# MLP down product: the running sums of seven chunks move from SBUF and VectorE to DRAM and accumulating DMAs

## The chip, the cores and the metric

The kernel runs on one core of a Trainium2 chip. The metric is the device time of one execution in microseconds (us); lower is better. Before the change the median of three runs was 2839.44 us (2832.86 to 2839.78).

Engines: PE is TensorE (matmuls, results in PSUM), DVE is VectorE, ACT is ScalarE, POOL is GpSimd, SP is SyncE, which here only issues DMAs. Every engine works through its own instructions in a fixed order; an instruction that waits holds back all behind it on that engine. A DMA is issued by an engine and lands later, while the engine goes on.

## The reference

Two layers, each a token mixer (mLSTM in layer 0, gated DeltaNet in layer 1), a cross-attention and an MLP, each wrapped as x + RMSNorm(f(RMSNorm(x))). There are 256 tokens of width 2048. The change lies in the MLP:

```python
D_MODEL = 2048; SEQ = 256; DEPTH = 2; D_FF = 4 * D_MODEL

def sq_relu_mlp(h, w_up, w_down):
    u = jax.nn.relu(h @ w_up)
    return (u * u) @ w_down

    # in reference(), for each layer i
        h = rms_norm(x, g[4])
        x = x + rms_norm(sq_relu_mlp(h, w_up[i], w_down[i]), g[5])
```

## The kernel before

**Numbers.** Products are made in float32r; weights and activations are split in two parts, hi and lo, and a product is hi x hi + hi x lo + lo x hi. For each piece of weights SP loads it to a raw tile, ACT casts it to `hi` (L154, L93, L94, L86) and DVE subtracts to get `lo` (L155, L82). These pieces are taken in a planned order (`Weights.plan`); each is called a unit here. Three units are kept: a unit's `hi` buffer is free when PE has ended the unit three before it. A unit of the down product is 4 x 128 rows by 512 columns of `w_down`: 12 matmuls for each of the two blocks of 128 tokens, 24 in all.

**The MLP** (`mlp`, L1132) cuts the 8192 features of the middle layer in NQ = 8 chunks. The up product of chunk 0 comes first (L1137). Then a loop over c = 1 to 7, called passes 1 to 7, does two things at once: the up product of chunk c (L1147 to L1153, eight feature blocks f) and the down product of chunk c - 1. The last chunk's down product stands behind the loop (`out_proj` in layer 0, `prod_tok` with `last` in layer 1).

The down product of a pass has two parts. For the first 1024 output columns it is a seven-product scheme for 2 x 2 blocks: seven products, `m0` to `m6`, each 128 x 512 in a PSUM bank of its own (five banks of tag "acc", two of tag "ps"), built up by L1164 to L1166 between the feature blocks. At f = 6 the first three are complete, at f = 7 the other four. For the other 1024 columns, `prod_tok("down", ..., 2, ...)` (L1178) makes an ordinary product: 2 column blocks x 2 token blocks, four banks, 4 units.

So each pass yields eleven 128 x 512 results, which are summed over the seven passes: in pass 1 ACT copies them to SBUF (L1170 for the seven, `Post.add` L616 for the four), in passes 2 to 7 DVE adds them from PSUM to SBUF (L1172, L616). The sums live in `y` (four tiles of two blocks, the eight blocks of the MLP's output) and in three tiles of tag "pair", which has three buffers. In pass 7 seven more additions on DVE (L1177) turn the seven sums into four output blocks. Behind the loop the last chunk's product is added to the same `y` blocks (L616), which are squared on ACT (L308), scaled and added to x.

The order on each engine is made by a scheduler from the order of the program and the dependencies.

Of the kernel before, what the change touches and what calls it, by code (L numbers as in the profile page):

```python
# [7 lines left out]
F32 = mybir.dt.float32  # L8
F32R = mybir.dt.float32r
AF = mybir.ActivationFunctionType  # L10
ALU = mybir.AluOpType
# [3 lines left out]
P = 128  # L15
# [165 lines left out]
def trunk(ctx: ExitStack, tc, x, mem, norm_g, mem_norm_g, w_mem_kv, w_xq, w_xo, w_up, w_down,  # L181
          mlstm_w_in, mlstm_b_gates, mlstm_head_g, mlstm_w_out, gdn_w_in, gdn_conv_w, gdn_a_log,
          gdn_dt_bias, gdn_norm_g, gdn_w_out, out):
    nc = tc.nc
    V, S, G, PE = nc.vector, nc.scalar, nc.gpsimd, nc.tensor
# [4 lines left out]
    tmp = ctx.enter_context(tc.tile_pool(name="tmp", bufs=2))  # L190
# [81 lines left out]
    def psum(name):  # L272
        return ps.tile([P, 512], F32, tag="ps", bufs=3, name=name)

    def acc(name):
        return ps.tile([P, 512], F32, tag="acc", bufs=5, name=name)
# [491 lines left out]
    first = []  # L768
# [239 lines left out]
    def out_proj(key, y, post, free, plus=False, more=None):  # L1008
        post.more = more
        prod_tok(key, y, 4, lambda ch, t, a: post.take(ch, t, a, plus), post=post, free=free)  # L1010
        return post.advance()
# [67 lines left out]
    def mlp_bias(rms):  # L1079

        s2 = small.tile([P, 2], F32, tag="s2", name="s2")
        V.tensor_scalar(s2, rms.sums(), 1.0 / D, EPS, ALU.mult, ALU.add)
        V.scalar_tensor_tensor(s2, s2, EPS, s2, ALU.mult, ALU.mult)
        return s2
# [47 lines left out]
    def mlp(l, lead):  # L1132
        mp_stack = ExitStack()
        mp = ws.tsum = mp_stack.enter_context(tc.tile_pool(name="mp", bufs=1))
        h = lead.h
        cur = Half(mp, 0, True)
        prod_feat("up", h, FK, cur.evac, lead=lead)  # L1137
        post = Post(l, 5, (1, 0) if l == 0 else None)
        y = post.y
        m = [tmp.tile([P, 512], F32, tag="pair", bufs=3, name=f"m{i}") for i in range(3)]  # L1140
        m1, m6, m7 = m
        c11, c21, c12, m5 = (y[ch][:, t, :] for ch in range(2) for t in range(2))
        kept = [m1, c11, c12, m5, m6, m7, c21]
        for c in range(1, NQ):
            nxt = Half(mp, c % 2, c < NQ - 1)
            banks = [acc(f"m{i}") for i in range(5)] + [psum(f"m{i}") for i in range(5, 7)]
            for f in range(FK):  # L1147
                hi, lo, nk, _ = ws.take("up")
                a = psum("up")
                for k in range(nk):  # L1150
                    PE.matmul(a, hi[k], h[k][:, :], start=(k == 0), stop=False, skip_group_check=True)  # L1151
                    PE.matmul(a[:, T:], lo[k], h[k][:, 0:T], start=False, stop=(k == nk - 1), skip_group_check=True)  # L1152
                nxt.evac(f, Bank(a, True))  # L1153
                j, part = f // 2, f % 2
                hi, lo, nf, _ = ws.take("down2")
                if part == 0:
                    lhs = [cur.block(2 * j, 0), cur.block(2 * j + 1, 0), cur.form(3, j)]
                    to = (0, 1, 2)
                else:
                    lhs = [cur.form(0, j), cur.form(1, j), cur.form(2, j), cur.block(2 * j + 1, 1)]  # L1160
                    to = (3, 4, 5, 6)
                for i in range(nf):
                    (sh, sl), a = lhs[i], banks[to[i]]
                    PE.matmul(a, sh, hi[i], start=(j == 0), stop=False)  # L1164
                    PE.matmul(a, sh, lo[i], start=False, stop=False)  # L1165
                    PE.matmul(a, sl, hi[i], start=False, stop=(j == FK // 2 - 1))  # L1166
                if j == FK // 2 - 1:
                    for i in to:
                        if c == 1:
                            S.copy(kept[i], banks[i])  # L1170
                        else:
                            V.tensor_tensor(kept[i], banks[i], kept[i], ALU.add)  # L1172
            if c == NQ - 1:
                for d, a, b, op in ((c11, c11, m1, ALU.add), (m6, m6, m1, ALU.add), (m7, m7, m6, ALU.add),
                                    (c21, m7, c21, ALU.subtract), (c12, c12, m6, ALU.add), (c12, c12, m5, ALU.add),
                                    (m5, m5, m7, ALU.add)):
                    V.tensor_tensor(d, a, b, op)  # L1177
            prod_tok("down", cur.u, 2, lambda ch, t, a: post.add(ch + 2, t, a, c == 1))  # L1178
            cur = nxt
        mp_stack.close()  # L1180
        u = cur.u
        post.bias = mlp_bias(lead.x_rms)
        if l == 0:
            return out_proj("down", u, post, (("h", 8), ("u", 0)), True)

        def last(ch, t, a):
            post.take(ch, t, a, True)
            if ch == 3:
                for i in range(4):
                    post.residual(i, t)  # L1190
                    (nc.sync if i % 2 else nc.scalar).dma_start(out[0, t * P : (t + 1) * P, i * 512 : (i + 1) * 512],
                                                                xk[i][:, t, :])

        prod_tok("down", u, 4, last, split=True)
# [446 lines left out]
    for l in range(2):  # L1641
        if l == 0:
            with tc.tile_pool(name="ml", bufs=2) as sc:
                y, post = mlstm(sc, h0, xrms, x_rest)
        else:
            ws.first = 400
            with tc.tile_pool(name="g0", bufs=1) as g0:
                y, post = gdn(g0, lead)
            ws.first = 0
        with tc.tile_pool(name="wx", bufs=1) as wx:  # L1650
            key, free = (("g_out", (("u", 8), ("u", 0))), ("m_out", (("h", 8), ("u", 0))))[l == 0]
            lead = out_proj(key, y, post, free, l == 1, wx)
            with tc.tile_pool(name="xa", bufs=2) as sc:
                lead = cross(sc, l, lead)
        lead = mlp(l, lead)
# [24 lines left out]
```

## Time and profile before

| What | Value |
|---|---|
| median of three runs | 2839.44 us (2832.86 to 2839.78) |
| the profiled execution | 2837.68 us, span 2835.9 us |
| granted PE clock | 0.997 |
| passes of layer 0 | 613 to 1161 us; a pass takes some 86 us |
| passes of layer 1 | end at 2784 us |
| HBM | 534.4 MB read, 25.2 MB written |

How to read it: the span goes from the first to the last instruction of the profiled execution; its own time holds some 2 us more. The page's share of an engine is an average over the run, so the stage that matters is looked at in windows. A row of a timeline has the start (us), the duration (us), the engine, the line, the operation and what it writes and reads; in brackets stands how long the engine was idle before and what ended that.

The weights use the DMA engines throughout the MLP:

```profile
q1 hardware_dynamic: 520000, 505.02, 58.8%
```

### The profile page before, as it was taken

What the parts mean: (1) busy time and instruction counts of PE and PEld (TensorE: products, weight loads), DVE (VectorE), ACT (ScalarE), POOL (GpSimd) and SP (SyncE); (2) the same over time, 40 slices, a digit from 0 to 9 for tenths busy, and PEclk for the clock granted to TensorE, in tenths of its full rate; (3) what the DMA queues carried; (4) which work ended last, traced back from release to release, by engine and by line L of the source; (5) the groups of instructions that cost most, each with busy time, mean ns of one, the idle gap of its engine ahead of it and who ended that gap; (6) DMA issues with size and microseconds to landing.
All of it is one profiled execution on the core that took longest, in us unless ns stands there. A gap on an engine that the chain in (4) does not pass through costs nothing.

```text
span 2835.9 us, 41595 instructions
## 1 busy us (share of the span) xinstructions
PE 2815.1 (99%) x15696; PEld 2396.1 (84%) x15696; DVE 2101.0 (74%) x3177; ACT 1672.4 (59%) x2603; POOL 170.4 (6%) x365
## 2 busy tenths in 40 slices
PE   9999999999999999999999999999999999999998
PEld 8888888888888888888888998888888888888887
DVE  6555657888888887787887895556578788888876
ACT  7444546776655566565765554544477666655663
POOL 0000000000000000002211114230000000000000
PEclk9999999999999999999999999999999999999999
DMA  8545565566666666757877778665654666666665
GB/s 281 181 147 176 193 200 165 169 194 195 198 196 195 199 189 195 227 155 232 244 220 222 213 209 276 200 202 194 204 178 151 211 184 202 193 193 193 195 194 168
DMA packets 537561, 562.34 MB, mean 198 GB/s; under 512 B 24672, under 2 KB 388016, under 8 KB 536080
## 3 DMA queue, kind: packets, MB, share of 16 engines
q1 hardware_dynamic: 520000, 505.02, 58.8%
q0 software_dynamic: 16464, 53.58, 5.8%
q8 instruction: 123, 2.02, 0.3%
q10 hardware_dynamic: 896, 1.09, 0.1%
q14 instruction: 78, 0.64, 0.1%
HBM read 534.38 MB, written 25.23 MB: 197 GB/s over the span
## 4 chain that ended last, share of the span: by engine, by line
PE 40%; DVE 6%; ACT 3%; DMA 2%; issue 2%; POOL 0%; DVEq 0%; ACTq 0%; POOLq 0%
PE up L1151 7%; PE up L1152 4%; DVE lo L155 2%; PE down L496 2%; PE down L497 2%; PE down L498 2%; PE g_out L497 2%; PE g_out L496 2%; PE g_out L498 2%; PE m L1165 2%; PE m L1164 2%; PE m L1166 2%; PE gz L496 1%; PE gz L498 1%; PE gz L497 1%
## 5 line engine op out<-in xcount | busy, mean ns | idle before, releaser
L155 DVE TENSOR_TENSOR lo<-raw,hi 128x1024 fp32r<-128x1024 f32 x812 | 966.3, 1220 | 327.7 <-ACT hi L154 324.9
L154 ACT CAST hi<-raw 128x1024 fp32r<-128x1024 f32 x812 | 827.1, 1047 | 479.6 <-PE down L498 96.7
L1151 PE MATMUL up<-h,hi 128*128 128x512 f32 x1792 | 636.9, 398 | 0.0
L1152 PE MATMUL up<-h,lo 128*128 128x256 f32 x1792 | 503.4, 281 | 0.4 <-DVE lo L155 0.4
L1151 PEld LDWEIGHTS up<-h,hi 128*128 128x128 f32 x1792 | 336.9, 188 | 82.4
L1152 PEld LDWEIGHTS up<-h,lo 128*128 128x128 f32 x1792 | 338.5, 189 | 5.3 <-DVE lo L155 0.8
L496 PE MATMUL down<-hi,u 128*128 128x512 f32 x576 | 224.2, 389 | 0.0
L497 PE MATMUL down<-lo,u 128*128 128x512 f32 x576 | 224.1, 389 | 0.0
L498 PE MATMUL down<-hi,u 128*128 128x512 f32 x576 | 224.1, 389 | 0.0
L82 DVE TENSOR_TENSOR lo<-tsum,hi 128x1024 fp32r<-128x1024 f32 x112 | 136.8, 1221 | 82.6 <-ACT hi L86 82.5
L86 ACT CAST hi<-tsum 128x1024 fp32r<-128x1024 f32 x112 | 117.6, 1050 | 131.9 <-PE up L1151 96.6
L496 PEld LDWEIGHTS down<-hi,u 128*128 128x128 f32 x576 | 108.1, 188 | 22.5
L498 PEld LDWEIGHTS down<-hi,u 128*128 128x128 f32 x576 | 108.1, 188 | 22.5
L497 PEld LDWEIGHTS down<-lo,u 128*128 128x128 f32 x576 | 108.1, 188 | 22.3
L93 ACT CAST hi<-raw 128x512 fp32r<-128x512 f32 x56 | 34.9, 623 | 121.6 <-PE up L1151 92.2
L1240 DVE SCALAR_TENSOR_TENSOR cv<-pad,cols,cv 128x256 f32<-128x256 f32 x192 | 92.5, 483 | 16.3 <-ACT cv L1238 12.4
L82 DVE TENSOR_TENSOR lo<-raw,hi 128x512 fp32r<-128x512 f32 x112 | 103.6, 955 | 0.0
L496 PE MATMUL gz<-hi,h 128*128 128x512 f32 x256 | 103.1, 403 | 0.0
L498 PE MATMUL gz<-hi,h 128*128 128x512 f32 x256 | 102.4, 400 | 0.0
L497 PE MATMUL gz<-lo,h 128*128 128x512 f32 x256 | 102.4, 400 | 0.0
L445 PE MATMUL gk<-h,hi 128*128 128x512 f32 x256 | 89.8, 395 | 0.0
L445 PE MATMUL gv<-h,hi 128*128 128x512 f32 x256 | 89.5, 394 | 0.0
(511 smaller groups left out, 6174.8 us busy)
## 6 DMA issues: line engine op xcount, KB each, us to landing
raw<-in_w_up SPq DMA_DIRECT2D x256, 512.0 KB, 4.7
raw<-in_w_down SPq DMA_DIRECT2D x256, 512.0 KB, 5.1
raw<-in_gdn_w_in SPq DMA_DIRECT2D x192, 512.0 KB, 4.9
raw<-in_mlstm_w_in SPq DMA_DIRECT2D x96, 512.0 KB, 4.0
raw<-in_gdn_w_out SPq DMA_DIRECT2D x64, 512.0 KB, 4.7
raw<-in_mlstm_w_out SPq DMA_DIRECT2D x32, 512.0 KB, 4.6
at_d<-at POOLq DMA_DIRECT2D x8, 1536.0 KB, 7.7
ab<-at_d POOLq DMA_DIRECT2D x16, 768.0 KB, 5.1
```

The source lines that it names most:

```text
L82: sub = lambda d, a, b: nc.vector.tensor_tensor(d, a, b, ALU.subtract)
L86: nc.scalar.copy(ht[:, j : j + 2, :], t[:, j : j + 2, :])
L154: a = nc.scalar.copy(h_, raw[:, :, :n])
L155: return a, nc.vector.tensor_tensor(l_, raw[:, :, :n], h_, ALU.subtract)
L445: PE.matmul(a, hi[k], srcs[k][:, :], start=(k == 0), stop=False, skip_group_check=True)
L496: PE.matmul(a, sh, hi[j], start=(kk == 0), stop=False)
L497: PE.matmul(a, sh, lo[j], start=False, stop=False)
L498: end[0] = PE.matmul(a, sl, hi[j], start=False, stop=(kk == nk - 1))
L1151: PE.matmul(a, hi[k], h[k][:, :], start=(k == 0), stop=False, skip_group_check=True)
L1152: PE.matmul(a[:, T:], lo[k], h[k][:, 0:T], start=False, stop=(k == nk - 1), skip_group_check=True)
L1164: PE.matmul(a, sh, hi[i], start=(j == 0), stop=False)
L1240: V.scalar_tensor_tensor(c, pad[:, j : j + T], w[j], c, ALU.mult, ALU.add)
```

## The change

The eleven sums are no longer kept in SBUF. In every pass ACT copies each result from its PSUM bank to a tile of tag "pair" (three buffers), and POOL issues a DMA from there to `sums_d[i]` in DRAM: a plain store in pass 1, one with `accum_op=ALU.add` in passes 2 to 7. Sums 0 to 6 are those of the seven products, 7 to 10 those of the ordinary product. In pass 7, after `prod_tok`, `Post` is made (before, it was made ahead of the loop), and eleven DMAs, issued by POOL, load the sums into `y` and into m1, m6 and m7, again tiles of tag "pair". The seven additions then run as before, but now stand behind `prod_tok`.

```diff
@@ mlp
-        post = Post(l, 5, (1, 0) if l == 0 else None)
-        y = post.y
-        m = [tmp.tile([P, 512], F32, tag="pair", bufs=3, name=f"m{i}") for i in range(3)]
-        m1, m6, m7 = m
-        c11, c21, c12, m5 = (y[ch][:, t, :] for ch in range(2) for t in range(2))
-        kept = [m1, c11, c12, m5, m6, m7, c21]
+        sums_d = tc.dram_tile([11, P, 512], F32, name="sums_d")
+
+        def keep(i, bank, first):
+
+            st = tmp.tile([P, 512], F32, tag="pair", bufs=3, name="kept")
+            S.copy(st, bank)
+            if first:
+                nc.gpsimd.dma_start(sums_d[i], st)
+            else:
+                nc.gpsimd.dma_start(sums_d[i], st, accum_op=ALU.add)
+
         for c in range(1, NQ):
...
                 if j == FK // 2 - 1:
                     for i in to:
-                        if c == 1:
-                            S.copy(kept[i], banks[i])
-                        else:
-                            V.tensor_tensor(kept[i], banks[i], kept[i], ALU.add)
+                        keep(i, banks[i], c == 1)
+            prod_tok("down", cur.u, 2, lambda ch, t, a: keep(7 + ch * 2 + t, a, c == 1))
             if c == NQ - 1:
+                post = Post(l, 5, (1, 0) if l == 0 else None)
+                y = [post.y[ch][:, t, :] for ch in range(4) for t in range(2)]
+                m = [tmp.tile([P, 512], F32, tag="pair", bufs=3, name=f"m{i}") for i in range(3)]
+                m1, m6, m7 = m
+                c11, c21, c12, m5 = y[:4]
+                for i, d in enumerate([m1, c11, c12, m5, m6, m7, c21] + y[4:]):
+                    nc.gpsimd.dma_start(d, sums_d[i])
                 for d, a, b, op in ((c11, c11, m1, ALU.add), (m6, m6, m1, ALU.add), (m7, m7, m6, ALU.add),
...
-            prod_tok("down", cur.u, 2, lambda ch, t, a: post.add(ch + 2, t, a, c == 1))
```

What it does to the engines' orders, at three places of layer 1's last pass. Names end in a running number; numbers of the same tile differ between the two programs. `hi` and `lo` carry the number of their unit: 520 to 523 are pass 7's ordinary product, 524 to 531 the product behind the loop. A wait on "DMASW" is one for a DMA that POOL issued, on "DMAHW" one for a DMA of SP.

First place: ACT, where pass 7's last four of the seven products are complete. Before:

```order
L154 CAST hi521_25816<-raw521_2_25814 128x1024 [waits DMAHW4_49,PE_49]
L1098 COPY both_25804<-up_25771 128x512 [waits PE_49]
L154 CAST hi521_25816<-raw521_0_25812 128x1024 [waits DMAHW3_49]
L1101 ACTIVATE j_up_25806<-j_up_25806 128x256 [waits DVE_49]
L1103 ACTIVATE u32_25590<-j_up_25806 128x256 [waits Activation_49]
L154 CAST hi522_25851<-raw522_0_25847 128x1024 [waits DMAHW5_49,PE_49]
L323 CAST u15_25250<-u32_25590 128x256 [waits Activation_49]
L154 CAST hi522_25851<-raw522_2_25849 128x1024 [waits DMAHW6_49]
```

And of the change:

```order
L154 CAST hi521_26109<-raw521_2_26107 128x1024 [waits DMAHW4_49]
L1143 COPY kept_26127<-m3_25541 128x512 [waits DMASW3_49,PE_49]
L1101 ACTIVATE j_up_26099<-j_up_26099 128x256 [waits DVE_49]
L1143 COPY kept_26130<-m4_25542 128x512 [waits DMASW4_49,PE_49]
L1103 ACTIVATE u32_25877<-j_up_26099 128x256 [waits Activation_49]
L1143 COPY kept_26133<-m5_25543 128x512 [waits DMASW5_49,PE_49]
L323 CAST u15_25537<-u32_25877 128x256 [waits Activation_49]
L154 CAST hi522_26145<-raw522_0_26141 128x1024 [waits DMAHW5_49,PE_49]
L1143 COPY kept_26136<-m6_25544 128x512 [waits DMASW0_49]
L154 CAST hi522_26145<-raw522_2_26143 128x1024 [waits DMAHW6_49]
```

Four copies have come into ACT's row, each with a wait for a DMA that frees its buffer; the last stands between the two halves of unit 522's cast. Passes 2 to 6 have the same pattern.

Second place: POOL in the same pass, from the accumulate of sum 6 on. Before, POOL had nothing to do in this MLP. Of the change:

```order
L1147 DMA sums_d_20825<-kept_26136 128x512 [waits Activation_49]
L1183 DMA y0_26291<-sums_d_20825 128x512 [waits DMASW4_49]
L1147 DMA sums_d_20825<-kept_26197 128x512 [waits DMASW6_49,Activation_49]
L1183 DMA y2_26293<-sums_d_20825 128x512 [waits DMASW7_49,DMASW6_49,DVE_49]
L1147 DMA sums_d_20825<-kept_26212 128x512 [waits Activation_49]
L1183 DMA y2_26293<-sums_d_20825 128x512 [waits DMASW1_49,DMASW0_49]
L1147 DMA sums_d_20825<-kept_26273 128x512 [waits DMASW2_49,Activation_49]
L1183 DMA m0_26300<-sums_d_20825 128x512 [waits DMASW3_49]
L1147 DMA sums_d_20825<-kept_26288 128x512 [waits Activation_49]
L1183 DMA m1_26301<-sums_d_20825 128x512 [waits DMASW5_49,DMASW2_49]
L1183 DMA y3_26294<-sums_d_20825 128x512 [waits DVE_49]
L1183 DMA m2_26302<-sums_d_20825 128x512 [waits DMASW7_49,DMASW4_49]
```

The loads (L1183) stand between the accumulates (L1147) of sums 6, 7, 8, 9 and 10. (m0, m1 and m2 are here m1, m6 and m7 of the code. Ahead of the piece stand the accumulates of sums 0 to 2, the loads of sums 1 and 2, the accumulates of sums 3 to 5 and the load of sum 3.) The loads of sums 1, 2, 3, 6, 7 and 8 each wait for the accumulate into the same sum, which has been issued just before or a few rows earlier; the load of m7 waits for the last accumulate, whose buffer it takes.

Third place: DVE at the product behind the loop. Before:

```order
L616 TENSOR_TENSOR y3_20662<-down1_1_25918,y3_20662 128x512 [waits PE_49]
L155 TENSOR_TENSOR lo526_26002<-raw526_0_25997,hi526_26001 128x1024 [waits DMAHW5_49,Activation_49]
L155 TENSOR_TENSOR lo526_26002<-raw526_2_25999,hi526_26001 128x1024 [waits DMAHW6_49,Activation_49]
L155 TENSOR_TENSOR lo527_26036<-raw527_0_26031,hi527_26035 128x1024 [waits DMAHW7_49,Activation_49]
L155 TENSOR_TENSOR lo527_26036<-raw527_2_26033,hi527_26035 128x1024 [waits DMAHW0_49,Activation_49]
```

And of the change:

```order
L155 TENSOR_TENSOR lo526_26334<-raw526_2_26331,hi526_26333 128x1024 [waits DMAHW6_49,Activation_49]
L1187 TENSOR_TENSOR y0_26291<-y0_26291,m0_26300 128x512 [waits DMASW6_49,DMASW3_49]
L1187 TENSOR_TENSOR m1_26301<-m1_26301,m0_26300 128x512 [waits DMASW4_49,DMASW5_49,DMASW2_49,DMASW7_49,DMASW1_49,DMASW0_49]
L1187 TENSOR_TENSOR y1_26292<-y1_26292,m1_26301 128x512 [waits DMASW7_49,DVE_49]
L1187 TENSOR_TENSOR y1_26292<-y1_26292 128x512 [waits DVE_49]
L1187 TENSOR_TENSOR m2_26302<-m2_26302,m1_26301 128x512 [waits DMASW6_49,DMASW7_49,DMASW4_49,DMASW1_49]
L155 TENSOR_TENSOR lo527_26368<-raw527_0_26363,hi527_26367 128x1024 [waits DMAHW7_49,Activation_49]
L1187 TENSOR_TENSOR y0_26291<-m2_26302,y0_26291 128x512 [waits DVE_49]
L1187 TENSOR_TENSOR y1_26292<-y1_26292,m2_26302 128x512
L155 TENSOR_TENSOR lo527_26368<-raw527_2_26365,hi527_26367 128x1024 [waits DMAHW0_49,Activation_49]
```

The seven additions, which stood among the splits of units 521 to 523, now stand between those of 526 and 527, and the one on m7 directly ahead of the first half of unit 527, the fourth unit of the product behind the loop.

## The prediction

> **What bounds the kernel now.** I read the page's first part, then the busy time of the engines in each pass of the MLP loop, then who PE waited for, then the timelines of ACT and DVE around the lines that change. The page and the windows say that PE (TensorE) is the bound; each window is one pass of the first layer's loop.
>
> ```profile
> PE 2815.1 (99%) x15696; PEld 2396.1 (84%) x15696; DVE 2101.0 (74%) x3177; ACT 1672.4 (59%) x2603; POOL 170.4 (6%) x365
> ...
> 700.00:786.00 86.00, 86.00 (x436) 72.71 (x436) 70.97 (x93) 52.00 (x75) 0.00 (x0) 1.00 0.65 196
> ...
> 959.00:1045.00 86.00, 86.00 (x437) 72.70 (x436) 71.02 (x93) 52.08 (x75) 0.00 (x0) 1.00 0.65 196
> ```
>
> The reader sees a pass of 86 us in which PE is busy for all 86, at a granted clock of 1.00, while DVE has 71 us, ACT 52 and POOL nothing. A busy PE need not be a fast one, so the waits decide. These are all that PE had in the up product, and its longest anywhere:
>
> ```profile
> PE l L1353 <- ACT l2sq L1349: 2.4, 2, 1.9
> ...
> PE up L422 <- ACT both L1098: 0.4, 1, 0.4
> PE up L1152 <- DVE lo L155: 0.4, 1, 0.4
> ```
>
> No line of the m or down products is in that answer. So DVE's work on the sums ends no wait of PE, and **taking it away can give back at most the 0.4 us** of L1152. The question is what the new waits cost.
>
> **The change, part by part.** The sums of before, in the answer that groups instructions by line (count, busy us, mean ns), under the split of the weights, which a later step needs:
>
> ```profile
> L155 DVE TENSOR_TENSOR lo<-raw,hi 128x1024 fp32r<-128x1024 f32 x808 | 962.5, 1222 | 325.7 <-ACT hi L154 322.9
> ...
> L616 DVE TENSOR_TENSOR y<-down,y 128x512 f32<-128x512 f32 x64 | 42.5, 688 | 8.0 <-PE down L498 8.0
> ...
> L1172 DVE TENSOR_TENSOR y<-m,y 128x512 f32<-128x512 f32 x48 | 31.9, 686 | 3.2 <-PE m L1166 3.1
> ...
> L1172 DVE TENSOR_TENSOR m<-m,m 128x512 f32<-128x512 f32 x36 | 23.9, 687 | 31.4 <-PE m L1166 31.4
> ```
>
> *DVE.* Passes 2 to 7 of both layers lose 7 + 4 additions of 0.69 us: 11 x 0.69 = 7.6 us a pass, 91 us in all, off the path. Gain: 0.
>
> *ACT, copies.* The same 11 banks are now copied by ACT. A copy of this shape took 0.59 us:
>
> ```profile
> L1170 ACT COPY y<-m x8: 585/592/612, 613.7 to 2246.3; 128x512 f32<-128x512 f32 x8
> ```
>
> That is 6.5 us more a pass, 52 to 58.5 of 86: hidden behind PE by itself.
>
> *ACT, waits.* The copies go through 3 buffers (tag "pair"), and a buffer is free when its DMA has landed. Call **L** the time from the issue of one accumulating DMA to its landing. ACT's order is in the rows of the section on the change, its times of before around pass 3 here:
>
> ```profile
> 784.67 1.05 ACT L86 CAST hi<-tsum 128x1024 fp32r<-128x1024 f32 x1
> 785.62 1.05 ACT L154 CAST hi<-raw 128x1024 fp32r<-128x1024 f32 x1
> ...
> 792.40 1.05 ACT L154 CAST hi<-raw 128x1024 fp32r<-128x1024 f32 x1
> 793.86 1.06 ACT L154 CAST hi<-raw 128x1024 fp32r<-128x1024 f32 x1 [0.41 <-PE m L1166]
> ...
> 804.74 1.05 ACT L154 CAST hi<-raw 128x1024 fp32r<-128x1024 f32 x1 [1.79 <-PE down L498]
> ```
>
> The first copy takes the place at 785.6 and is done at 786.2. The fourth stands behind the cast of 792.4, so at 793.4: it waits for the first one's DMA only if L is over 7.1. The seventh needs the fourth one's buffer: 794.0 + 0.1 + L, 800.6 at L = 6.5. Behind it on ACT stands the second half of a cast (1.05), then DVE's split (1.22, row of L155): with the copy, 803.5. PE finishes a unit at 804.7 and starts the one that these weights belong to; their half is read half a unit later (a unit takes 5.44, last rows of this part), at 807.4. Margin 4 us, cost 0. Over L = 7.1 both waits add up: 786.3 + 2L + 0.7 + 2.9 passes 807.4 at L = 8.8, and beyond that each pass loses 2 x (L - 8.8).
>
> *The size of L.* No accumulating DMA is in this trace. The nearest rows are the software queue's (POOLq) transfers:
>
> ```profile
> grow<-g_d POOLq DMA_DIRECT2D x16, 256.0 KB, 5.5
> z_d<-zst POOLq DMA_DIRECT2D x8, 256.0 KB, 5.1
> ...
> tn_d<-tnt POOLq DMA_DIRECT2D x2, 512.0 KB, 6.5
> ```
>
> From below, a plain store of the same 256 KB from SBUF to DRAM: 5.1. From above, a load and a store one after the other: 5.5 + 5.1 = 10.6. An accumulate reads 256 KB from SBUF and 256 KB from DRAM and writes 256 KB; of the rows it is nearest to the store of 512 KB, so I take **L = 6.5**.
>
> The software queue's row on the page (packets, MB, share of 16 engines' span) bears on this:
>
> ```profile
> q0 software_dynamic: 16464, 53.58, 5.8%
> ```
>
> 53.58 MB in 5.8% of 16 x 2835.9 us is 20 GB/s a DMA engine, so 256 KB over 16 engines is 0.8 us of moving. The Trainium skill, "Collectives: The Full Stack", section Part 3, says of a reducing transfer that its add costs no cycles but needs two source reads, which halves its rate. By that L would be 5.1 + 0.8 = 5.9, an estimate (by the formula below the sum would be 2844.3); no run here shows an accumulate yet.
>
> *The end of the loop* is where L is multiplied. In pass 7 POOL's queue holds, by the rows in the section on the change, accumulates and loads in turn, and a load of sum i waits until the accumulate into sum i has landed. POOL works in order, so the next accumulate is not issued before that. Times of layer 1:
>
> ```profile
> 2753.34 1.05 ACT L86 CAST hi<-tsum 128x1024 fp32r<-128x1024 f32 x1
> 2754.29 1.05 ACT L154 CAST hi<-raw 128x1024 fp32r<-128x1024 f32 x1
> 2755.24 0.42 ACT L1101 ACTIVATE j_up<-j_up 128x256 f32<-128x256 f32 x1
> ...
> 2784.29 2.01 ACT L154 CAST hi<-raw 128x1024 fp32r<-128x1024 f32 x2 [2.60 <-PE down L498]
> 2789.73 2.00 ACT L154 CAST hi<-raw 128x1024 fp32r<-128x1024 f32 x2 [3.43 <-PE down L498]
> ```
>
> Three copies with two activations of 0.42 between them, from 2754.3 on: ACT starts each some 0.1 before the last one's end, as these rows do, so the third is done at 2756.7 and its accumulate issued at 2756.8. Then, link by link: sums 2, 3, 6, 7, 8 and 10 each have to land before POOL or the buffers let the next one go, which makes **6 L**. Between landing and next issue lies the issue of the load that waited, 0.56 (POOL's time for one, row below) plus 0.1: four times 0.65; behind sum 8 come three issues, 1.75.
>
> ```profile
> L1395 POOL DMA_DIRECT2D z_d<-zst x8: 547/560/567, 1282.3 to 1531.8; - x8
> ```
>
> Last the load of m7 lands, 5.5 (row of grow). Sum: 2756.8 + 6L + 4.35 + 5.5 = 2766.6 + 6L. DVE has the addition on m7 (0.69) and right behind it the split of the fourth unit's first half (1.22, row of L155): ready at 2768.5 + 6L. PE ends pass 7 at 2784.3 (the row's release) and takes a unit every 5.44 (2789.73 - 2784.29), so it needs the fourth at 2784.3 + 16.3 = 2800.6. **PE stalls for 6L - 32.1**: 0 at L = 5.35, 6.9 us at 6.5. What follows (two additions, the other half, then the late additions of L616 and the squares on ACT) keeps to the same delay or less. Layer 0 has the same queue and the same distances. Two tails: 13.8 us.
>
> *Edits at nothing.* `Post` moves, but its gain loads stand at the same places of SP's queue. m's first three PSUM banks are read out by 788 (three copies from 785.6 on); the down product, which takes them again, begins only when m ends, at the release of 793.9. The traffic grows by 11 transfers a pass; hidden as the third rival says.
>
> **Sum.** The profiled execution took 2837.7 (span 2835.9, 1.8 around it); the median of the three runs is 2839.4, 0.1% above. 2837.7 + 0 (passes) + 13.8 (tails) = **2851.5 us**, 0.5% slower. About 0.3%, 8.5 us, is what a measurement of this kernel can tell from no change; the tails reach it at L = 6.06.
>
> **Rivals.**
> 1. *The landings are quick and nothing shows* (not slower). Deciding point: L under 5.35, then both tails are covered and the time is 2837.7; up to 6.06 it stays within 0.3%. For it: the plain store's 5.1, which lies under the point. Against it: the second read. Beside this: the Trainium skill, "DMA: Bandwidth & Descriptors", section Anatomy of one DMA, gives 2.0 us + bytes/436 GB/s for a transfer of the software queue, 2.6 us here, an estimate, by which the time is 2837.7; the row of z_d, 5.1, disagrees and I go by the row. 0.39.
> 2. *ACT is held in every pass.* Deciding point: L over 8.8. At 10.6 the tails cost 2 x 31.5 = 63 and ten passes (2 to 6, twice) 3.6 each: 2837.7 + 63 + 36 = 2937. At 8.8 it begins with 2879. For it: L is unknown, and the seven sums of m come within 10 us on 3 buffers. Against: it needs 3.7 us over the plain store. 0.10.
> 3. *The added traffic makes the weight loads late.* Against it, the weights' landings in a stretch where the software queue was busy and in one where it was not (first the state matrices' stage, then the passes), which differ by 0.1:
>
> ```profile
> raw<-in_gdn_w_in SPq DMA_DIRECT2D x153, 512.0 KB, 5.0
> ...
> raw<-in_w_down SPq DMA_DIRECT2D x84, 512.0 KB, 5.1
> ```
>
> It needs weights that come over 4 us late (the margin above); a stall of 1 us in 12 passes gives 2850 before the tails. 0.02.
> 4. *Faster*, if PE is slowed by DVE's reads of PSUM in a way that no wait shows. No row speaks for it; 1% off would be 2809. 0.02.
>
> That the change does not do what it says is excluded by the rows of the order: DVE's additions are gone, ACT and POOL have the copies and DMAs.
>
> **How the numbers follow.** The forecast, tails that cost by L between 6.06 and 8.8 and passes that cost nothing, has 0.47; its time is that of L = 6.5. Slower by over 0.3%: 0.47 + 0.10 + 0.02 = 0.59. Within 0.3%: 0.39. Faster: 0.02. The range goes from rival 1 (2837.7, less 3 for the scatter of the runs shown) into rival 2, to L = 9.3 (2 x 23.7 for the tails, ten passes of 1.0: 2895), since L is only bounded: 2835 to 2895; outside lie half of rival 2 and rival 4, 0.07, and as much again for a chain that I may have read wrongly.
>
> **What would show it.** The landing of L1147 on POOL's queue gives L at once. In passes 2 to 6 PE shows no wait, while ACT waits for a DMA before L1143's seventh copy (some 1 us at 6.5). In both tails PE waits for DVE's split L155 in the down product, and DVE sits before L1187 until m7's load; that wait is 6L - 32.1. PE waiting in every pass would mean rival 2; no wait in the tails, rival 1; a wait that starts at the weights' DMA, rival 3. The forecast fails if POOL issues the accumulates faster than one after the other, or if their landing varies much along the chain.

## The result: 0.9% slower, and the profile after

Over four runs each, the changed kernel took 2861.64 us (2861.49 to 2863.98) and the kernel before 2838.78: a ratio of 1.0088, with a 95% interval from 1.0076 to 1.0100. The profiled execution has a span of 2859.8 us against 2835.9, 23.9 us more, where the prediction had 13.8.

The first part of the page, the software queue's row, and the same two windows over passes of layer 0 as before:

```profile
PE 2821.0 (99%) x15696; PEld 2399.7 (84%) x15696; DVE 2029.7 (71%) x3045; ACT 1735.8 (61%) x2735; POOL 310.6 (11%) x541
...
q0 software_dynamic: 38992, 99.73, 14.5%
...
700.00:786.00 86.00, 86.00 (x436) 72.71 (x435) 65.06 (x83) 57.41 (x85) 9.57 (x11) 1.00 0.85 229
959.00:1045.00 86.00, 86.00 (x436) 72.72 (x435) 65.07 (x83) 57.28 (x85) 9.63 (x11) 1.00 0.84 229
```

The work moved as the diff says (DVE 71 to 65 us a pass, ACT 52 to 57, POOL 0 to 9.6), and PE is busy for all of the 86 us at a clock of 1.00. The DMA engines' share rises from 0.65 to 0.85. So the passes cost nothing, and the 23.9 us lie elsewhere. Next, whom PE waited for (us in total, times, longest):

```profile
PE down L497 <- DVE lo L155: 12.6, 3, 6.2
PE lth L679 <- DVE xs L661: 4.7, 4, 3.7
```

Before, the first was not there and the second was short:

```profile
PE lth L679 <- DVE xs L661: 1.4, 4, 0.5
```

The first row is the stall of the tails that was forecast, 12.6 us in all; the second has 3.3 us more than before, all of it in one wait of 3.7 at the end of layer 0. Together that is 16 us of 23.9. (A third new wait, 2.6 us in layer 1's token mixer, adds nothing: from layer 0's last transpose to the first up matmul of layer 1's loop it took 966 us, and 967 before.) For the rest one measures the tails whole, from the start of the last up matmul to that of the last down matmul and, in layer 0, on to the last transpose of L679. The rows by line, first of before, then of after, end in the first and last start:

```profile
L1151 PE MATMUL up<-h,hi x76: 389/398/404, 1099.7 to 1135.9; 128*128 128x512 f32 x76
L498 PE MATMUL down<-hi,u x96: 388/389/390, 1139.5 to 1204.1; 128*128 128x512 f32 x96
L679 PE MATMUL lth<-ident,xs x16: 272/273/329, 1204.9 to 1213.1; 128*128 128x128 f32 x16
...
L1151 PE MATMUL up<-h,hi x122: 389/398/404, 2699.9 to 2759.2; 128*128 128x512 f32 x122
L498 PE MATMUL down<-hi,u x96: 388/389/390, 2762.8 to 2827.4; 128*128 128x512 f32 x96
```

```profile
L1156 PE MATMUL up<-h,hi x76: 389/398/403, 1099.8 to 1136.0; 128*128 128x512 f32 x76
L498 PE MATMUL down<-hi,u x96: 387/389/628, 1139.6 to 1213.1; 128*128 128x512 f32 x96
L679 PE MATMUL lth<-ident,xs x16: 271/344/446, 1217.2 to 1227.4; 128*128 128x128 f32 x16
...
L1156 PE MATMUL up<-h,hi x128: 389/398/403, 2711.5 to 2772.9; 128*128 128x512 f32 x128
L498 PE MATMUL down<-hi,u x114: 388/389/628, 2699.7 to 2851.3; 128*128 128x512 f32 x114
```

Layer 0's tail grew from 68.2 to 77.1 us, layer 1's from 68.2 to 78.4, and from the last down matmul to the last transpose layer 0 took 14.3 in place of 9.0: 8.9 + 10.2 + 5.3 = 24.4, the whole difference within 0.5. The tails grew by more than PE waited in them, and the longest matmul in the rows of after is 628 ns where it was 390. The windows around layer 0's stall say why (length, PE busy, granted clock, DMA share, GB/s):

```profile
1174.00:1177.00 3.00, 3.00 (x15) 1.00 0.96 210
1177.00:1182.00 5.00, 0.88 (x4) 1.00 0.65 212
1182.00:1184.00 2.00, 0.33 (x1) 0.56 0.00 0
1184.00:1189.00 5.00, 5.00 (x13) 0.50 0.60 193
1189.00:1191.00 2.00, 2.00 (x10) 0.98 0.73 212
```

PE stands still from 1177.9 to 1183.7. At about 1182 its granted clock falls to 0.50, and it stays there until 1189, though PE is busy again from 1183.7: 13 matmuls in 5 us, where 3 us held 15 before. The same comes behind layer 1's stall and behind the wait for L661. **A stall costs its length and then some 3 us lost at half speed**, which the prediction's sum did not have.

### The profile page after: what moved, and what is told of

It is laid out like the page before. It is cut to its first block, busy times and chain, and to the rows that moved or that the text cites. A ratio compares the mean times of both kernels' runs of the same rounds, so it can differ in the third digit from the quotient of the medians.

```text
span 2859.8 us, 42143 instructions
## 1 busy us (share of the span) xinstructions
PE 2821.0 (99%) x15696; PEld 2399.7 (84%) x15696; DVE 2029.7 (71%) x3045; ACT 1735.8 (61%) x2735; POOL 310.6 (11%) x541
## 3 DMA queue, kind: packets, MB, share of 16 engines
q0 software_dynamic: 38992, 99.73, 14.5%
## 4 chain that ended last, share of the span: by engine, by line
PE 39%; DVE 6%; ACT 3%; DMA 3%; issue 2%; POOL 0%; DVEq 0%; ACTq 0%; POOLq 0%
PE up L1156 7%; PE up L1157 4%; DVE lo L155 2%; PE down L497 2%; PE g_out L497 2%; PE down L498 2%; PE down L496 2%; PE g_out L498 2%; PE g_out L496 2%; PE m L1170 2%; PE m L1169 2%; PE m L1171 2%; PE gz L498 2%; PE gz L496 1%; PE gz L497 1%
## 5 line engine op out<-in xcount | busy, mean ns | idle before, releaser
L155 DVE TENSOR_TENSOR lo<-raw,hi 128x1024 fp32r<-128x1024 f32 x812 | 967.0, 1221 | 409.5 <-ACT hi L154 407.0
L497 PE MATMUL down<-lo,u 128*128 128x512 f32 x576 | 226.9, 394 | 12.6 <-DVE lo L155 12.6
L1147 POOL DMA_DIRECT2D sums_d<-kept x132 | 116.6, 983 | 878.8 <-ACT kept L1143 701.0
L497 PEld LDWEIGHTS down<-lo,u 128*128 128x128 f32 x576 | 109.4, 190 | 37.2 <-DVE lo L155 14.3
L497 PE MATMUL gz<-lo,h 128*128 128x512 f32 x256 | 102.7, 401 | 0.0
```

Source lines behind the costliest of these rows:

```text
L155: return a, nc.vector.tensor_tensor(l_, raw[:, :, :n], h_, ALU.subtract)
L497: PE.matmul(a, sh, lo[j], start=False, stop=False)
L1147: nc.gpsimd.dma_start(sums_d[i], st, accum_op=ALU.add)
```

## The experiments

Twelve kernels, in four questions: what makes the stall, what follows a stall, what the wait at the end of layer 0 is, and whether the sums can be read elsewhere. Times are medians, with ratios to runs of the kernel before on the same chip; "tail" is the length defined above (68.2 before), and "layer 0's end" reaches from the last up matmul to the last transpose of L679 (77.2 before, 91.4 after).

### What makes the stall

**loads_last** orders POOL's queue anew:

```diff
-                nc.gpsimd.dma_start(sums_d[i], st, accum_op=ALU.add)
+                stored.append(nc.gpsimd.dma_start(sums_d[i], st, accum_op=ALU.add))
...
-                    nc.gpsimd.dma_start(d, sums_d[i])
+                    behind(nc.gpsimd.dma_start(d, sums_d[i]), *stored[-11:])
```

> The change with one more rule: on POOL's queue each of a layer's 11 loads of sums (L1183) stands behind that layer's last accumulate (L1147). Theory A (the cost is the chain of landings in the tail: accumulates and loads alternate on POOL's in-order queue, so 6 landings come one after the other, PE stalls, and behind the stall its granted clock is 0.5 for some 6.7 us): the accumulates come three at a time (3 buffers), four landings instead of six, m7 lands about 10 us earlier, PE's waits for L155 in the down product fall from 12.6 us to under 1.5, no window of the tail has a clock under 1.00, and the time is within 0.3% of before (2830 to 2847 us). Rival B (the added traffic or the accumulates themselves hold the weights back): the order on POOL changes little, PE still waits 5 us or more in a tail, time over 2852.

Measured: 2853.67 us, ratio 1.0057 (1.0045 to 1.0069). PE's waits for L155 fell from 12.6 to 4.4 us and the tails to 70.4 and 72.5, so the order was most of the stall; but L661's wait grew to 5.5, and theory A missed on the waits, on the clock of layer 1's tail (below) and by 7 us on the time. Part of my expectation was wrong for a reason in the code: the copies of sums 9 and 10 are made only when the pass's last product ends (their accumulates issued at 1164.6 and 1165.1), and m7 needs one of the three buffers that those copies hold, so its load could issue no sooner than 1172.8, against 1178.2 in the change.

**plain_store** keeps the order and drops the accumulation, so that it leaves out the adding of the chunks' products:

```diff
-                nc.gpsimd.dma_start(sums_d[i], st, accum_op=ALU.add)
+                nc.gpsimd.dma_start(sums_d[i], st)
```

> The change with plain stores in place of the accumulates; it leaves out the adding of the chunks' products. Queue order, copies, loads and combinations are those of the change. Theory A: a landing takes 5.5 us and an issue 0.54 us (L1145 in the trace of the change) instead of 6.7 and 0.90, so the chain of 6 is some 7 to 9 us shorter; PE waits under 1.5 us in each tail, too short for the clock to fall; time 2836 to 2847. Rival C (it is the order alone, whatever is queued): both tails keep 4 us or more of wait, time over 2848.

Measured: 2855.26 us, ratio 1.0064 (1.0051 to 1.0078), tails 75.4 and 72.9, layer 0's end 90.2. Rival C it was: PE still waited 4.9 us in layer 0 and 4.1 in layer 1, 9.0 of the 12.6. The issue did fall to 0.54 us, but the landing did not keep to the 5.5 that I had taken from L1145: in this tail its median was 6.9 (1135 to 1150) and 7.7 (1150 to 1170). The order makes the chain, with or without an accumulation.

The same run prices the accumulation. At the same places a plain store landed in 5.6 us and an accumulate in 6.7. For the same 99.73 MB the software queue's packets took 10.2% of 16 engines' span here, and 14.5% in the change:

```profile
q0 software_dynamic: 30544, 99.73, 10.2%
```

Over the 132 transfers that differ, (14.5% x 2859.8 - 10.2% x 2852.6) / 132 is 0.9 us more of every DMA engine for an accumulate, with 64 more packets; a plain transfer's packets take 0.7 us (10.2% x 2852.6 less 5.8% x 2835.9 before, over 176 transfers).

**own_buffers** removes both ties, the order and the shared buffers:

```diff
-                m = [tmp.tile([P, 512], F32, tag="pair", bufs=3, name=f"m{i}") for i in range(3)]
+                m = y[4:7]
...
-                for i, d in enumerate([m1, c11, c12, m5, m6, m7, c21] + y[4:]):
-                    nc.gpsimd.dma_start(d, sums_d[i])
+                for i, d in enumerate([m1, c11, c12, m5, m6, m7, c21]):
+                    behind(nc.gpsimd.dma_start(d, sums_d[i]), stored[-3])
...
+                for i, d in enumerate(y[4:]):
+                    behind(nc.gpsimd.dma_start(d, sums_d[7 + i]), stored[-1])
```

> The change with its tail mended in two ways: m1, m6 and m7 are loaded into y's tiles of channels 2 and 3 instead of the 3 buffers that the copies need, and on POOL's queue the loads of sums 0 to 6 stand behind the ninth accumulate, those of sums 7 to 10 behind the eleventh. Copies, accumulates and loads are as many as in the change. Theory A (only the chain of landings costs): the loads issue from about 1157 in layer 0, m7 lands near 1166 instead of 1183, DVE is free of the combinations by 1170; from the last matmul of the last up product to the last of the down product it is 68.2 us in both layers as before the change (77.1 and 78.3 in the change), no PE wait over 1 us in the tails, L661's wait under 1.5, time within 0.3% of before. Rival B (the 8.7 MB more of traffic in a layer's passes and tail cost something by themselves): tails of 72 us and more or longer passes, time over 2848.

Measured: 2850.67 us, ratio 1.0043 (1.0027 to 1.0059). The stall is gone: tails 68.2 and 68.9, PE's wait for L155 0.4 us in all. That settles the stall: as many copies, accumulates and loads, and no stall, once no accumulate stands behind a load that waits and no load needs a buffer of the copies. (The traffic in the expectation is too small: the software queue moved 99.73 - 53.58 = 46 MB more, 23 in each layer.) Yet the time is only half way back, and theory A missed on it, since L661's wait is now the longest of all:

```profile
PE lth L679 <- DVE xs L661: 8.5, 4, 6.8
...
PE down L497 <- DVE lo L155: 0.4, 1, 0.4
```

Layer 0's end took 85.2, 8.0 more than before, and layer 1's tail 0.7 more. The medians differ by 11.5; the other 2.8 lie in neither place and stay open (the stretch from layer 0's last transpose to the first up matmul of layer 1's loop, which no edit touches, took 960 to 971 us from one profiled execution to another, 971 in this one).

### What follows a stall

Four kernels (and two more below) are the one before the change with nothing added but one long DVE instruction, whose result nobody reads. hold14, hold19 and hold24 ran first; hold8 was sized from their waits:

```diff
+                if l == 1:
+                    hold = small.tile([P, 24], F32, tag="hold", bufs=1, name="hold")
+                    V.tensor_reduce(hold, m1.unsqueeze(1).to_broadcast([P, 24, 512]), AX.X, ALU.add)
             prod_tok(
```

> As hold14 with 8 x 512 elements (about 4.4 us). By hold14, 19 and 24 (waits 5.6, 8.3 and 11.0, one row of 512 for each 0.54) PE waits 2.4 us. If the clock falls only behind waits of 3.4 us or more, it stays 1.00 and the tail of layer 1 grows from 68.2 by 2.4; if it may fall behind shorter ones, as behind the 2.4 us in layer 1 of loads_last, it grows by 4 to 5.4.

> The kernel before the change, with one more DVE instruction near the end of layer 1's pass 7, a reduction of 14 x 512 elements (about 7.5 us) that nobody reads; no DMA is added. It delays DVE's next splits of the weights, so that PE waits. Theory A: a short wait, 0 to 3 us, after which the granted clock stays 1.00; the span grows by the wait alone. Rival E (the half clock behind the stalls comes from the DMA traffic): the clock stays 1.00 in this and in the longer ones as well.

> As hold14 with 19 x 512 elements (about 10 us). Theory A: a wait of 2 to 5 us, near the point where the clock falls; if it falls to 0.5 behind the wait, the span grows by 1 to 3 us more than the wait. Rival E: clock 1.00, span longer by the wait.

> As hold14 with 24 x 512 elements (about 12.8 us). Theory A: a wait of 5 to 8 us and then a clock of 0.5 for 5 to 7 us of PE's work, so that the span grows by 2.5 to 3.5 us more than the wait. Rival E: clock 1.00, span longer by the wait.

The tail of layer 1 in each, with PE's one wait in it; single runs, so the time of the whole kernel is not compared:

| kernel | PE's wait, us | layer 1's tail, us | tail less 68.2 less the wait |
|---|---|---|---|
| hold8 | 2.5 | 70.9 | 0.2 |
| hold14 | 5.6 | 76.8 | 3.0 |
| hold19 | 8.3 | 79.5 | 3.0 |
| hold24 | 11.0 | 82.1 | 2.9 |

The first three waits to be measured came out some 3 us over the longest that theory A had (0 to 3, 2 to 5 and 5 to 8), and hold14 lost the clock that it was to keep. Behind all three PE ran at half speed, with no DMA added. The windows of hold24:

```profile
2762.00:2764.00 2.00, 1.99 (x9) 1.00 0.00 0
2764.00:2774.00 10.00, 0.00 (x0) 0.65 0.00 0
2774.00:2780.00 6.00, 5.04 (x12) 0.50 0.79 237
2780.00:2782.00 2.00, 2.00 (x9) 0.86 0.98 357
```

So the half clock belongs to PE's idleness (rival E falls), and costs 3 us whether the wait was 5.6 or 11 us. Between hold8 and hold14 lies a limit that is not sharp. hold8's wait kept the clock; a wait no longer than that, in layer 1 of loads_last, lost it for some 3.4 us, a cost of 1.9 (tail 72.5). The first row and the second are hold8's, the wait and the stretch behind it; then the same of loads_last:

```profile
2770.79 0.50 PE L497 MATMUL down<-lo,u 128*128 128x512 f32 x1 [2.49 <-DVE lo L155]
...
2771.00:2772.00 1.00, 1.00 (x5) 1.00 0.97 313
```

```profile
2821.42 0.79 PE L497 MATMUL down<-lo,u 128*128 128x512 f32 x1 [2.41 <-DVE lo L155]
...
2821.00:2825.00 4.00, 3.58 (x9) 0.57 0.88 234
```

Other waits went both ways. Two further down, 2.6 us in traffic_layer0 and 3.4 in hold_late_layer0, lost the clock and cost 1.7 and 2.8 us more than their length. But plain_store's longer wait in layer 1, 3.5 us, kept it. These are PE's waits there and the windows from that wait on:

```profile
PE down L497 <- DVE lo L155: 4.1, 2, 3.5
...
2812.00:2814.00 2.00, 0.68 (x4) 1.00 0.76 234
2814.00:2816.00 2.00, 0.00 (x0) 1.00 0.02 6
2816.00:2818.00 2.00, 1.66 (x6) 1.00 0.32 80
```

In the trace's record of the clock, each stretch at 0.50 behind such a wait lasts 3.41 us or a whole multiple of it: 3.41 in layer 1 of loads_last and in traffic_layer0, 6.83 in the change, 10.24 in hold19, 13.65 in hold24.

The Trainium skill, "TensorE: Matmul & The Clock Gate", section Part 1, has this mechanism: a gate that halves PE's clock after an idle window of about 3.4 us and frees it after a busy one, the windows running on by themselves. The trace agrees in the length of the slow stretch: 6.83 us (1182.26 to 1189.09) are two such windows, one that still holds the end of the wait and one that is busy throughout. It does not agree in the limit, since a wait of 2.4 us was enough once. Where a wait falls in windows that run on by themselves might be what decides between 2.4 us lost and 3.5 kept; that was not tried.

### The wait at the end of layer 0

**hold24_layer0** and **hold_late_layer0** put the long DVE instruction into layer 0, the first where hold24 has it, the second three units on:

> As hold24, in layer 0. Theory A: a wait of 5 to 8 us, a clock of 0.5 behind it, and, because the loads of the weights stood still meanwhile, a second PE wait of 2 us or more for L661 at the layer's end, as in the change. Rival F (the second wait comes from the accumulates' and loads' traffic): no second wait over 1 us.

> The kernel before the change with a DVE reduction of 28 x 512 elements (about 15 us) in layer 0, three units further on than hold24_layer0's, where the combinations stand in the change; no DMA is added. It should stop PE for 5 to 9 us in the down product. Theory G (the second wait, at L661, is what is left of a late hold of DVE: the loads of the weights issue late behind it and four units are too few to catch up): L661's longest wait is 2 us or more. Rival F (that wait needs the change's traffic): L661 at most 1.0, as in hold24_layer0.

Measured: waits of 11.0 and 3.4 us in the down product (5 to 8 and 5 to 9 expected), tails 82.0 and 74.4, and L661's longest wait 1.0 in both; hold8, which adds nothing to layer 0, has 1.2. So theories A and G missed, and neither of these holds of DVE makes a second wait. That does not exclude theory G for the change: hold_late_layer0's hold ended at 1172.3, 41 us ahead of the last down matmul, while in the change DVE came back to its splits at 1182.4, 31 us ahead of it, some two units nearer to the end.

**traffic_layer0** adds the traffic alone to the kernel before:

```diff
+                if l == 0:
+                    extra = tc.dram_tile([12, P, 512], F32, name="extra")
+                    last_ = None
+                    for b in range(4):
+                        for op in ({}, dict(accum_op=ALU.add)):
+                            for i in range(b * 3, b * 3 + 3):
+                                x_ = nc.gpsimd.dma_start(extra[i], m1, **op)
...
```

> The kernel before the change with traffic alone added in the tail of layer 0: 12 stores of 256 KB and 12 accumulates into the same places on POOL's queue, three and three, from m1, which nobody waits for; no engine but POOL has more to do. Theory H (the tail's traffic makes the weights' loads land late, and that is the second wait, at L661): landings of in_w_down rise from about 5 to 6 us and more between 1135 and 1180, L661's longest wait is 2 us or more, while the down product waits little. Rival G (it is the hold of DVE by the combinations): L661 at most 1.2, as before the change.

Measured: L661's wait 1.4, so theory H missed as I put it; 1.4 is hardly more than hold8's 1.2. But its first half holds: the weights land late. The rows of DMA issues between 1150 and 1170 (count, KB, median us to landing), of before, of own_buffers and of traffic_layer0:

```profile
raw<-in_w_down SPq DMA_DIRECT2D x10, 512.0 KB, 5.4
```

```profile
raw<-in_w_down SPq DMA_DIRECT2D x7, 512.0 KB, 9.2
y<-sums_d POOLq DMA_DIRECT2D x9, 256.0 KB, 9.7
sums_d<-kept POOLq DMA_DIRECT2D x4, 256.0 KB, 7.9
```

```profile
raw<-in_w_down SPq DMA_DIRECT2D x8, 512.0 KB, 8.2
extra<-m POOLq DMA_DIRECT2D x9, 256.0 KB, 9.0
```

And here that traffic stopped PE in the down product itself, for 2.6 us at L155 (tail 72.5), with no engine but POOL given more to do; ahead of that ACT's cast had waited 4.2 us for a load of in_w_down. What joins these kernels is how far the split weights are ahead of PE when the layer ends. For the last but one unit of the down product, the time from the end of the split of its first half to PE's first use of it (each from the trace's rows of L155 and L497), beside L661's wait:

| kernel | lead of the last but one unit, us | L661's wait, us |
|---|---|---|
| before | 8.6 | 0.4 |
| hold24_layer0 | 8.6 | 1.0 |
| hold_late_layer0 | 8.6 | 1.0 |
| traffic_layer0 | 8.6 | 1.4 |
| after | 6.0 | 3.7 |
| plain_store | 5.4 | 5.0 |
| loads_last | 5.0 | 5.5 |
| own_buffers | 3.6 | 6.8 |

A stall of PE that comes early enough gives the stream of weights its lead back, as I read the second to fourth rows. In own_buffers PE does not stop in this tail: the lead was down to 0.7 us three units before the last, grew to 3.1 and 3.6, and what lacked was paid at the layer's end. There the next layer's weights are late as well (the first load of in_gdn_w_in issued 19.0 us ahead of the last down matmul before, 14.0 in own_buffers), their splits stand on DVE ahead of L616 and with it of L661, and PE has nothing else to do. That reading fits all eight rows; it was not tried apart, for instance with the same traffic ended earlier.

What takes the lead away need not be the same in each. In own_buffers the weights of 1150 to 1170 landed in 9.2 us. In the change they landed in 5.5, much as before (5.4), but no load of in_w_down was issued between 1167.3 and 1183.6, while DVE stood before the additions, waiting for m1, m6 and m7. There the late hold of DVE, theory G's cause, fits better than the traffic; no run separates the two.

### Versions without the tail's transfers

**loads_early** loads the sums at the start of pass 7 and adds that pass's products on DVE as before the change; **loads_early_2** has the loads behind pass 6's last accumulate:

```diff
+            if c == NQ - 1:
+                return V.tensor_tensor(dst[i], bank, dst[i], ALU.add)
...
+            if c == NQ - 1:
+                post = Post(l, 5, (1, 0) if l == 0 else None)
...
+                for i, d in enumerate(dst):
+                    behind(nc.gpsimd.dma_start(d, sums_d[i]), stored[-1])
```

> The sums of passes 1 to 6 are kept in DRAM as in the change, but loaded at the start of pass 7, where DVE adds pass 7's products out of PSUM as before the change. No load waits for an accumulate issued near it. Theory A: the passes cost nothing and there is no chain at the end: no PE wait over 1 us in the tails, time within 0.3% of before (2830 to 2847). Rival D (copies and accumulates in the passes cost something that no wait of PE shows): 2848 or more, as five sixths of the added copies and DMAs remain.

> As loads_early, but on POOL's queue all loads of the sums stand behind the last accumulate of pass 6, so that no accumulate waits behind a load and no copy on ACT waits for an accumulate that POOL holds back. The tail has no DMA of sums at all. Theory A and H (the chain and the tail's traffic are what costs; copies and accumulates in the passes cost nothing): passes of 86.3 us as before, pass 7 without the 1 to 2 us waits of loads_early, both tails 68.2, L661's longest wait under 1.2 us, time within 0.3% of before. Rival D (copies and accumulates in the passes cost something no wait shows): passes over 86.5 us, time 2848 or more.

Measured: 2845.21 us, ratio 1.0032 (1.0019 to 1.0045), and 2850.47 us, ratio 1.0054 (1.0033 to 1.0075). In both the two tails are 68.2 (68.1 in layer 1) and L661's longest wait is under 0.8: the tail is mended, and PE is busy throughout passes 1 to 6. loads_early_2's time lies where rival D had it, but the passes that rival D would charge cost nothing. The cost sits in pass 7 (the last up matmul starts 4.0 and 2.5 us later in loads_early's two layers, 7.0 and 3.8 in loads_early_2's, counted from the loop's first). In loads_early_2 the 11 loads leave within 10 us (1079 to 1089); PE's waits, ACT's longest one behind these loads, and the landings between 1078 and 1100:

```profile
PE up L1167 <- ACT both L1098: 7.2, 3, 4.0
...
1091.16 1.05 ACT L154 CAST hi<-raw 128x1024 fp32r<-128x1024 f32 x1 [4.89 <-DMA raw<-in_w_up]
...
raw<-in_w_up SPq DMA_DIRECT2D x4, 512.0 KB, 9.9
y<-sums_d POOLq DMA_DIRECT2D x8, 256.0 KB, 8.9
raw<-in_w_down SPq DMA_DIRECT2D x2, 512.0 KB, 12.7
```

The weights land late again; ACT, which works in order, waits for them and copies out the bank that PE needs 4 us too late. Neither version reaches the time of the kernel before; none that was tried does.

## Why the prediction was right, and where its sum was short

- **Side and place: right.** The time lies in the range, slower, and the cost in the tails of both layers. Gain from DVE nothing, copies hidden behind PE: the windows show both (5.9 us a pass left DVE and 5.4 came to ACT where 7.6 and 6.5 were added up, as rows that follow at once overlap by 0.1; neither bears on the time). But the range also held no change and more than twice the cost, so that lying in it shows little; the 13.8 us are 10 short.
- **ACT's waits in the passes: right in kind.** ACT did wait before its copies (us in total, times, longest):

```profile
ACT kept L1143 <- DMA sums_d<-kept: 50.8, 19, 6.3
```

 In passes 1 to 6 the longest of these waits is 1.8 to 3.8 us, where "some 1 us" was forecast, and PE did not notice. In pass 7 a copy of m waited 5.5 us in layer 0 and 6.3 in layer 1, and PE's wait of 0.6 in layer 1 (2789.3) follows behind it.
- **L: taken as 6.5, measured 6.7**, nearest to the row of the store of 512 KB. That the bytes are the reason rests on this one number. The other estimate, 5.9, added one more moving of 0.8 us to a store of 5.1; plain_store shows 0.9 more of moving and 1.1 more of landing, so the step was about right and the store under it too quick (5.6 at these places). The rows of L1147 and of its landings:

```profile
L1147 POOL DMA_DIRECT2D sums_d<-kept x132: 850/896/1602, 700.2 to 2809.6; - x132
...
DMA to landing us min/median/max: 3.9/6.7/11.9
```

- **The chain: right, by two errors that cancel.** POOL's timeline in layer 0's tail shows it, a load that waits for an accumulate (in brackets), and the next accumulate straight behind the load:

```profile
1149.42 0.57 POOL L1183 DMA_DIRECT2D y<-sums_d  x1 [5.96 <-DMA sums_d<-kept]
1149.98 0.90 POOL L1147 DMA_DIRECT2D sums_d<-kept  x1
1155.52 0.57 POOL L1183 DMA_DIRECT2D y<-sums_d  x1 [4.64 <-DMA sums_d<-kept]
1156.08 0.90 POOL L1147 DMA_DIRECT2D sums_d<-kept  x1
1163.87 0.57 POOL L1183 DMA_DIRECT2D y<-sums_d  x1 [6.89 <-DMA sums_d<-kept]
1164.43 0.90 POOL L1147 DMA_DIRECT2D sums_d<-kept  x1
...
1178.20 0.54 POOL L1183 DMA_DIRECT2D m<-sums_d  x1 [0.79 <-DMA sums_d<-kept]
```

 In layer 1 the addition on m7 was forecast for 2766.6 + 6L = 2805.6, or 2819.3 with the 13.7 us by which that tail began later; it started at 2819.8 (last start of m on L1187). But the six links, each from the issue of an accumulate to that of the load that it held back, took from 5.0 to 9.2 us there and 41.9 in all, where the sum has 6 x 6.5 = 39; and the addition came 3.4 us behind the issue of m7's load, where the sum has 5.5. The landings thus varied along the chain as the prediction feared, and their sum came out near. own_buffers and loads_last each cut the chain in another way, and the stall shrank with it.
- **The stall: 6.9 us forecast, 5.8 and 6.2 measured** (12.6 in all with the 0.6 of layer 1 named above). This is the term that the prediction rested on, and it is right. What failed is the step from the stall to the time, "two tails: 13.8 us": it took a stall to cost its own length. Each cost 3 us more at a granted clock of 0.50, 6.5 us in all (8.9 + 10.2 less 12.6), and the hold kernels show the same loss with no DMA added.
- **"What follows … keeps to the same delay or less": wrong in layer 0**, by 5.3 us between the last down matmul and the last transpose: 3.3 of added wait for L661, and 2 more at half clock behind it. Layer 1 has nothing behind its tail, and it kept to the delay.
- **Rival 3, late weights: put at 0.02, and partly true.** I set it against the landings of two stages with an ordinary load. In the tail they were 8.6 us (1135 to 1150) where the kernel before had 4.8 in the same window, with the accumulates bunched beside them. traffic_layer0 shows that such traffic alone delays the weights and stops PE; own_buffers shows some 8 us of layer 0's end left when the stall is gone.

## What to carry to other kernels

Where producers and consumers share one in-order queue, count the landings that its order puts in a row; give the consumers' destinations buffers of their own and issue them behind the last producer. Price a stall of PE of some 5 us or more at its length plus about 3 us for the half clock behind it, allow for up to as much behind one of 2.4 to 3.5 us, and look one stage further than the stall: a lead that was used up is paid where PE next has nothing queued. Traffic that is free as a mean over a pass may still bunch where the weights' lead is thinnest.

## Not expected of the hardware

- An accumulating DMA of 256 KB from SBUF to DRAM lands in 6.7 us (3.9 to 11.9), a plain store of the same in 5.5 (5.6 at the accumulates' places), and its issue holds POOL for 0.85 to 1.6 us where the plain one takes 0.54 (rows of L1147 and L1145, and of L1147 in plain_store).
- PE's granted clock fell to 0.50 some 2.0 to 5.2 us into an idle stretch and came back 3 to 6 us after work resumed, in steps of 3.41 us; of two waits of 2.4 and 2.5 us the shorter lost it, and one of 3.5 kept it.
- With accumulates, stores or loads of the software queue bunched beside them, the weights' loads of 512 KB landed in up to 9.9 us (medians of the windows above; 12.7 for two loads) in place of 5.
